# Weight sums and low parts of the first ConvGLU: VectorE subtractions replaced by adding transfers issued by GpSimd

## The chip, the cores and the metric

The kernel runs on one core of one Trainium2 chip. The core has five engines that execute their own instruction lists and wait for each other by semaphores: TensorE (PE in the profile; PEld is its weight load), VectorE (DVE), ScalarE (ACT), GpSimd (POOL) and SyncE (SP), which here only issues transfers. Sixteen DMA engines carry out the transfers. The metric is the device time of one execution in microseconds (us).

## What is computed

The reference is a two-layer model over 512 latent tokens and 256 context tokens of width 1024. Layer 0 mixes tokens by attention, layer 1 by a gated recurrence; each layer ends with a ConvGLU. The change touches the ConvGLU of layer 0, which works on latent and context tokens:

```python
def conv_glu(h, w_up, conv_w, conv_b, w_down):
    gate, val = jnp.split(h @ w_up, 2, axis=-1)
    return (jax.nn.silu(dwconv3(gate, conv_w, conv_b)) * val) @ w_down
```

`w_up` is 1024 x 5632: its first 2816 columns give the gate, the others the value. `dwconv3` is a convolution over three neighbouring tokens. All is float32.

## The kernel before

Every float32 product is made of three products in TensorE's faster float32r format. An operand x is split into a high part, x rounded to float32r, and a low part, x minus the high part; high x high, high x low and low x high are added up in PSUM.

The columns of the ConvGLU are worked through in 22 blocks of 128 (`ft` in `up`, L973). One block needs 128 gate columns and 128 value columns of `w_up`, a pair. With the 1024 rows cut into two halves, the weights of a pair are four blocks: a11 and a12 (gate, first and second half), a21 and a22 (value). The activations are four blocks as well, two halves of the width by two halves of the tokens. The 2 x 2 by 2 x 2 block product is done with seven block products in place of eight, in the manner of Strassen and Winograd: seven sums or differences of weight blocks are multiplied by seven sums or differences of activation blocks (`hs`, prepared once in `combos`, L384), and `gate_pair` (L914) adds the seven results up to the four output blocks. Each block product (`product`, L181) is 12 matmuls of 128 x 128 by 128 x 386.

`load_pair` (L125) prepares the weights of a pair. `load_raw` (L90) issues two transfers on SP's queue, gate and value, into a raw tile `wr` of 128 x 2048. Inside, the nested `total` (L135) makes the four sums s1 to s4 on VectorE, mostly in place in the raw tile, and the nested `parts` (L139) splits each of the seven operands: ScalarE rounds to the high part `wh` (L140), VectorE subtracts to the low part `wl` (L141). Each block is 128 x 512.

Three stocks of tiles set the pace of preparation:

- the raw tiles: two (`wp`, L1306). The weights of the pairs, the weights of the down projection (four transfers a round) and the weights of the conditioning of layer 1 (`wada`, one tile per pair in most pairs, `ada_steps`) take turns in them.
- the operand tiles: six of `wh` and six of `wl` in this stage (four in `ws0`, two in `wsC`), shared by the seven operands of a pair and the operands of the down projection (`load_w`, L99).
- one tile for s1.

The 22 blocks run in six rounds of 3, 4, 4, 4, 3 and 4 (`ROUNDS`). A round first does `up` for its blocks and for the first block of the next round, then the down projection of its blocks: eight output tiles of 128 rows, six matmuls per block and output tile (three products, latent and context tokens apart). After its products, a block is finished on VectorE and ScalarE (convolution, SiLU), with one product with the row factors on GpSimd (L926, `gg` times `R`). The order of the work within each engine is not the program's order: a planner at compile time simulates the program with its own durations and writes a fixed list for every engine, by readiness and priority (`high_priority`, `W_AHEAD`). On the chip each engine executes its list in order.

Of the kernel before, what the change touches and what calls it, by code (L numbers as in the profile page):

```python
# [8 lines left out]
F32 = mybir.dt.float32  # L9
F32R = mybir.dt.float32r  # L10
BF16 = mybir.dt.bfloat16
AF = mybir.ActivationFunctionType
ALU = mybir.AluOpType
# [3 lines left out]
P = 128  # L17
# [51 lines left out]
def f(t):  # L69
    return t.bitcast(F32)  # L70


class Kernel:
# [25 lines left out]
    def load_w(self, parts, cols=False):  # L99
# [23 lines left out]
        return out  # L123

    def load_pair(self, parts, tmp):  # L125


        nc = self.nc
        raw, n = self.load_raw(parts)
        q = n // 4  # L130
        a11, a12, a21, a22 = (raw[:, i * q:(i + 1) * q] for i in range(4))
        s1 = tmp.tile([P, 512], F32, tag="s1", name="s1")[:, 0:q]
        ops = [tuple(t[:, 0:q] for t in self.operand()) for _ in range(7)]

        def total(o, x, y, op):  # L135
            nc.vector.tensor_tensor(o, x, y, op=op)
            return o

        def parts(i, src):  # L139
            nc.scalar.activation(ops[i][0], src, AF.Copy)  # L140
            nc.vector.tensor_tensor(ops[i][1], src, f(ops[i][0]), op=ALU.subtract)  # L141


        with self.tc.high_priority(offset=W_AHEAD):
            parts(0, a11)
            parts(1, a12)
            total(s1, a21, a22, ALU.add)
            s3 = total(a21, a11, a21, ALU.subtract)
            s2 = total(a11, s1, a11, ALU.subtract)
            parts(3, s2)  # L150
            parts(6, s3)
            parts(2, s1)
            parts(5, a22)
            s4 = total(a12, a12, s2, ALU.subtract)
            parts(4, s4)
        return ops

    def wcols(self, w, lo, n):
# [225 lines left out]
    def combos(self, ys, kk, hs, late=False):  # L384

        nc = self.nc
        (b11, b12), (b21, b22) = ys

        def put(i, src):
            nc.scalar.activation(hs[i][:, 0, kk], src, AF.Copy)  # L392
            nc.vector.tensor_tensor(hs[i][:, 1, kk], src, f(hs[i][:, 0, kk]), op=ALU.subtract)

        def diff(o, x, y, eng=nc.vector):
            eng.tensor_tensor(o, x, y, op=ALU.subtract)
            return o

        if late:
            t3 = diff(b22, b22, b12)  # L400
            t4 = diff(b21, b21, b11, nc.gpsimd)
            put(5, diff(b21, t4, t3))
            put(6, t3)
            return
        put(0, b11)
        put(1, b21)
        put(4, b22)
        t1 = diff(b12, b12, b11)
        put(2, t1)
        t2 = diff(b22, b22, t1)  # L410
        put(3, t2)
        yield
        put(5, diff(b21, b21, t2))
        put(6, diff(b11, t2, b11))

    def shifts(self, l, w, hn):
# [497 lines left out]
    def gate_pair(self, ft, ops, hs, G, gg, R, rows, half, tmp, bank):  # L914


        nc = self.nc
        Z, Y, V = (bank(x)[:, 0:half] for x in ("pZ", "pY", "pV"))

        def prod(i, ps, first=False):  # L920
            self.product(ps, ops[i], lambda k: (hs[i][:, 0, k], hs[i][:, 1, k]), 4, first)

        g = (G[:, 1:1 + half], G[:, 1 + half:1 + 2 * half], gg[:, 0:half], gg[:, half:])
        t0, t2 = (tmp.tile([P, half], F32, tag="t", name="t", bufs=2) for _ in range(2))
        add = lambda o, x, y: nc.vector.tensor_tensor(o, x, y, op=ALU.add)  # L925
        times = lambda eng, o, x, y: eng.tensor_tensor(o, x, y, op=ALU.mult)  # L926

        prod(0, Z, True)
        nc.scalar.activation(t0, Z, AF.Copy)
        prod(1, Y, True)  # L930
        add(g[0], t0, Y)
        prod(3, Z)
        nc.scalar.activation(g[2], Z, AF.Copy)
        next(rows, None)
        if ft == 0:
            prod(2, Z)
            nc.scalar.activation(t2, Z, AF.Copy)
            prod(4, Z)
            prod(6, V, True)
            nc.scalar.activation(g[3], V, AF.Copy)  # L940
            prod(5, V)
        else:
            prod(6, V, True)
            nc.scalar.activation(g[3], V, AF.Copy)
            prod(2, Z)
            nc.scalar.activation(t2, Z, AF.Copy)
            prod(5, V)
            prod(4, Z)
        add(g[3], g[3], t2)
        add(g[2], g[2], V)  # L950
        for _ in rows:
            pass

        times(nc.vector, g[0], g[0], R[:, 0:half])
        times(nc.vector, g[1], Z, R[:, half:])
        times(nc.gpsimd, gg, gg, R)
# [496 lines left out]
```

## Time and profile before

| | us |
|---|---|
| median of 3 runs | 1871.61 |
| lowest and highest | 1870.25 and 1875.65 |
| profiled execution | 1872.88 |
| its span, from first to last instruction | 1871.1 |
| first ConvGLU, in the profile | about 446 to 985 |

The page of the profile has six parts: busy time by engine, the span in 40 slices, DMA queues, the chain of work that ended last, the costliest groups of instructions, and DMA issues. The trace behind it answers narrower questions, in the same wording: busy time by windows, groups of instructions in a window, who waited for whom (us in total, times, longest), instructions in order of time. A group's row gives line, engine, operation, output <- inputs, shapes and count, then busy us and mean ns of one, then the engine's idle time before them and what ended it. Busy time of TensorE is modelled, and a few records of matmuls and of other instructions are missing. The slices show where the stages are; the first ConvGLU takes the tenth to the twenty-first.

```profile
PE   6999999998999999999998999999998999999998
...
DVE  5575667466867686766777676777676655455462
ACT  4354555465534252434354333333332443233332
POOL 1233333103201000101013101111110200000000
```

### The profile page before, as it was taken

What the parts mean: (1) busy time and instruction counts of PE and PEld (TensorE: products, weight loads), DVE (VectorE), ACT (ScalarE), POOL (GpSimd) and SP (SyncE); (2) the same over time, 40 slices, a digit from 0 to 9 for tenths busy, and PEclk for the clock granted to TensorE, in tenths of its full rate; (3) what the DMA queues carried; (4) which work ended last, traced back from release to release, by engine and by line L of the source; (5) the groups of instructions that cost most, each with busy time, mean ns of one, the idle gap of its engine ahead of it and who ended that gap; (6) DMA issues with size and microseconds to landing.
All of it is one profiled execution on the core that took longest, in us unless ns stands there. A gap on an engine that the chain in (4) does not pass through costs nothing.

```text
span 1871.1 us, 32302 instructions
## 1 busy us (share of the span) xinstructions
PE 1801.3 (96%) x13326; PEld 1576.9 (84%) x13326; DVE 1214.1 (65%) x2243; ACT 754.7 (40%) x1478; POOL 247.4 (13%) x233
## 2 busy tenths in 40 slices
PE   6999999998999999999998999999998999999998
PEld 4976786787888888989887888988886799899997
DVE  5575667466867686766777676777676655455462
ACT  4354555465534252434354333333332443233332
POOL 1233333103201000101013101111110200000000
PEclk9999999998999999999998999999999999999999
DMA  9204104232333333233313212122220332333321
GB/s 309 66 23 158 47 24 169 68 102 68 124 113 102 113 124 113 91 113 124 113 61 90 58 35 58 35 57 58 57 69 24 90 91 91 90 96 96 92 82 65
DMA packets 204416, 166.44 MB, mean 89 GB/s; under 512 B 5149, under 2 KB 198254, under 8 KB 199150
## 3 DMA queue, kind: packets, MB, share of 16 engines
q1 hardware_dynamic: 196608, 160.47, 27.8%
q10 hardware_dynamic: 7662, 3.92, 0.7%
q8 instruction: 105, 1.72, 0.4%
q14 instruction: 41, 0.34, 0.1%
HBM read 162.27 MB, written 2.10 MB: 88 GB/s over the span
## 4 chain that ended last, share of the span: by engine, by line
PE 87%; DVE 5%; DMA 4%; issue 2%; ACT 1%; POOL 1%; SPq 0%; ACTq 0%; POOLq 0%; DVEq 0%
PE dn L170 15%; PE pd L170 13%; PE pZ L188 8%; PE pf L170 8%; PE pV L188 4%; PE pjq L598 4%; PE pv L170 4%; PE ao L170 4%; PE ho L170 3%; PE pq L170 3%; PE pv L824 2%; PE pt L816 2%; PE ada L309 2%; PE pY L188 2%; PE pgate L170 2%; PE kv L598 2%
## 5 line engine op out<-in xcount | busy, mean ns | idle before, releaser
L117 ACT ACTIVATE wh<-wr 128x512 fp32r<-128x512 f32 (+1 forms) x320 | 193.0, 618 | 452.3 <-DMA wr<-in_ffn_w_up 74.8
L118 DVE TENSOR_TENSOR wl<-wr,wh 128x512 fp32r<-128x512 f32 (+1 forms) x320 | 223.6, 705 | 140.3 <-ACT wh L117 138.3
L170 PE MATMUL dn<-g,wh 128*128 128x512 f32 (+1 forms) x1056 | 263.3, 357 | 2.2 <-ACT g L995 2.2
L170 PE MATMUL pd<-hn,wh 128*128 128x256 f32 (+1 forms) x1408 | 227.3, 284 | 0.9 <-issue 0.9
L170 PEld LDWEIGHTS dn<-g,wh 128*128 128x128 f32 x1056 | 175.4, 189 | 32.7 <-ACT g L995 2.8
L170 PEld LDWEIGHTS pd<-hn,wh 128*128 128x128 f32 x1408 | 194.2, 190 | 2.5 <-issue 2.3
L188 PE MATMUL pZ<-hs,wh 128*128 128x386 f32 x704 | 185.2, 345 | 3.0 <-ACT wh L140 1.5
L170 PE MATMUL dn<-g,wl 128*128 128x512 f32 (+1 forms) x528 | 159.4, 356 | 0.0
L140 ACT ACTIVATE wh<-wr 128x512 fp32r<-128x512 f32 x132 | 81.6, 628 | 167.9 <-DMA wr<-in_ffn_w_up 47.4
L170 PE MATMUL pd<-hn,wl 128*128 128x256 f32 x704 | 141.8, 283 | 0.0
L188 PEld LDWEIGHTS pZ<-hs,wh 128*128 128x128 f32 x704 | 128.0, 190 | 15.7 <-ACT wh L140 4.4
L141 DVE TENSOR_TENSOR wl<-wr,wh 128x512 fp32r<-128x512 f32 x132 | 94.0, 717 | 53.6 <-ACT wh L140 53.5
L170 PE MATMUL pf<-hn,wh 128*128 128x512 f32 (+1 forms) x512 | 119.3, 349 | 9.7 <-DVE xc L1023 8.8
L188 PE MATMUL pZ<-hs,wl 128*128 128x386 f32 x352 | 119.4, 343 | 2.2 <-DVE wl L141 2.2
L926 POOL TENSOR_TENSOR gg<-gg,R 128x772 f32<-128x772 f32 x22 | 53.9, 2449 | 458.3 <-DVE gg L925 446.6
L170 PEld LDWEIGHTS pd<-hn,wl 128*128 128x128 f32 x704 | 109.0, 190 | 0.0
L1023 DVE SCALAR_TENSOR_TENSOR xl<-dn,mod,xl 128x512 f32<-128x512 f32 x72 | 53.9, 748 | 73.7 <-PE dn L170 73.6
L170 PEld LDWEIGHTS dn<-g,wl 128*128 128x128 f32 x528 | 87.4, 188 | 14.8
L170 PEld LDWEIGHTS pf<-hn,wh 128*128 128x128 f32 x512 | 80.9, 192 | 22.5 <-ACT wh L117 9.1
L188 PE MATMUL pV<-hs,wh 128*128 128x386 f32 x352 | 92.2, 341 | 5.0 <-ACT hs L392 5.0
L598 PE MATMUL pjq<-wh,hn 128*128 128x256 f32 x384 | 77.8, 291 | 0.0
L188 PEld LDWEIGHTS pZ<-hs,wl 128*128 128x128 f32 x352 | 66.7, 190 | 6.6 <-DVE gg L925 3.4
(299 smaller groups left out, 3807.1 us busy)
## 6 DMA issues: line engine op xcount, KB each, us to landing
wr<-in_ffn_w_up SPq DMA_DIRECT2D x88, 512.0 KB, 5.1
wada<-in_ada_w SPq DMA_DIRECT2D x40, 1024.0 KB, 4.8
wr<-in_hgrn_w_in SPq DMA_DIRECT2D x40, 512.0 KB, 4.2
ar<-in_ada_w SPq DMA_DIRECT2D x32, 256.0 KB, 7.1
wr<-in_ffn_w_down SPq DMA_DIRECT2D x16, 512.0 KB, 4.1
wr<-in_ffn_w_down SPq DMA_DIRECT2D x8, 896.0 KB, 4.7
wr<-in_attn_w_in SPq DMA_DIRECT2D x6, 1024.0 KB, 8.1
wr<-in_attn_w_out SPq DMA_DIRECT2D x8, 512.0 KB, 4.9
```

The costliest lines, as they stand in the source:

```text
L117: nc.scalar.activation(wh, src, AF.Copy)
L118: nc.vector.tensor_tensor(wl, src, f(wh), op=ALU.subtract)
L140: nc.scalar.activation(ops[i][0], src, AF.Copy)
L141: nc.vector.tensor_tensor(ops[i][1], src, f(ops[i][0]), op=ALU.subtract)
L170: nc.tensor.matmul(o, lhsT=wt, rhs=at[:, t0:t0 + o.shape[1]], start=(first and n == 0 and i == 0), stop=(last and n == len(ks) - 1 and i = ...
L188: self.nc.tensor.matmul(ps, lhsT=wt, rhs=at, start=(first and k == 0 and i == 0), stop=(k == nk - 1 and i == 2), skip_group_check=not first)
L309: nc.tensor.matmul(ps[32 * j:32 * j + 32, 0:512], lhsT=self.cs[:, k, :], rhs=raw[:, j * 512:(j + 1) * 512], start=(k == 0), stop=(k == KT ...
L598: nc.tensor.matmul(out, lhsT=x, rhs=y[:, wk], start=(start and k == 0 and j == 0), stop=(stop and k == KT - 1 and j == 2))
L816: nc.tensor.transpose(pt[:, j * P:(j + 1) * P], pr[j][:, b * P:(b + 1) * P], self.ident)
L824: nc.tensor.matmul(pv[a * HD:(a + 1) * HD, 0:256], lhsT=V[:, tl, g, :], rhs=pT[:, a * 256:(a + 1) * 256], start=(b == 0), stop=(b == len(t ...
L926: times = lambda eng, o, x, y: eng.tensor_tensor(o, x, y, op=ALU.mult)
L1023: nc.vector.scalar_tensor_tensor(x[:, d], o, self.modc(l, v, 5, d), x[:, d], op0=ALU.mult, op1=ALU.add)
```

## The change

`load_pair` no longer uses VectorE. A low part is made in two steps: ScalarE writes the negated high part into `wl` (a Copy with scale -1), and a transfer issued by GpSimd adds the source block to it in place (`dma_start` with `accum_op=ALU.add`). The four sums are adding transfers as well: s3 = a11 + a21 in a tile of its own, which is seeded by a further load of the a11 block from memory on SP's queue; s1 = a21 + a22 in a21; s2 = a11 + s1 in a11; s4 = a12 + s2 in a12. Since a transfer can only add, some of the sums have other signs than before. The signs are made good elsewhere: in `combos` some activation blocks are differences the other way round or are split with a sign of -1 (the low part with `scalar_tensor_tensor` there), and `gate_pair` copies two results with scale -1 and subtracts in place of adding.

```diff
     def load_pair(self, parts, tmp):
...
-        s1 = tmp.tile([P, 512], F32, tag="s1", name="s1")[:, 0:q]
+        s3 = tmp.tile([P, 512], F32, tag="s1", name="s3")[:, 0:q]
         ops = [tuple(t[:, 0:q] for t in self.operand()) for _ in range(7)]
 
-        def total(o, x, y, op):
-            nc.vector.tensor_tensor(o, x, y, op=op)
+        def more(o, x):
+            nc.gpsimd.dma_start(out=o, in_=x, accum_op=ALU.add)
             return o
 
-        def parts(i, src):
+        def parts_(i, src):
             nc.scalar.activation(ops[i][0], src, AF.Copy)
-            nc.vector.tensor_tensor(ops[i][1], src, f(ops[i][0]), op=ALU.subtract)
+            nc.scalar.activation(ops[i][1], f(ops[i][0]), AF.Copy, scale=-1.0)
+            more(ops[i][1], src)
 
         with self.tc.high_priority(offset=W_AHEAD):
-            parts(0, a11)
-            parts(1, a12)
-            total(s1, a21, a22, ALU.add)
-            s3 = total(a21, a11, a21, ALU.subtract)
-            s2 = total(a11, s1, a11, ALU.subtract)
-            parts(3, s2)
-            parts(6, s3)
-            parts(2, s1)
-            parts(5, a22)
-            s4 = total(a12, a12, s2, ALU.subtract)
-            parts(4, s4)
+            nc.sync.dma_start(out=s3.rearrange("p (k m) -> p k m", m=P), in_=parts[0][:, 0:4])
+            parts_(0, a11)
+            parts_(1, a12)
+            more(s3, a21)
+            s1 = more(a21, a22)
+            s2 = more(a11, s1)
+            parts_(3, s2)
+            parts_(6, s3)
+            parts_(2, s1)
+            parts_(5, a22)
+            s4 = more(a12, s2)
+            parts_(4, s4)
         return ops
...
-        def put(i, src):
-            nc.scalar.activation(hs[i][:, 0, kk], src, AF.Copy)
-            nc.vector.tensor_tensor(hs[i][:, 1, kk], src, f(hs[i][:, 0, kk]), op=ALU.subtract)
+        def put(i, src, sign=1.0):
+            nc.scalar.activation(hs[i][:, 0, kk], src, AF.Copy, scale=sign)
+            if sign > 0:
+                nc.vector.tensor_tensor(hs[i][:, 1, kk], src, f(hs[i][:, 0, kk]), op=ALU.subtract)
+            else:
+                nc.vector.scalar_tensor_tensor(hs[i][:, 1, kk], src, sign, f(hs[i][:, 0, kk]), op0=ALU.mult, op1=ALU.subtract)
...
-        put(2, t1)
+        put(2, t1, -1.0)
...
-        put(3, t2)
+        put(3, t2, -1.0)
...
-        nc.scalar.activation(g[2], Z, AF.Copy)
+        nc.scalar.activation(g[2], Z, AF.Copy, scale=-1.0)
...
-        add(g[3], g[3], t2)
-        add(g[2], g[2], V)
+        less(g[3], t2)
+        less(g[2], V)
```

More of the change, by code (lines that the diff above doesn't have):

```diff
@@ L401, in combos @@
             t4 = diff(b21, b21, b11, nc.gpsimd)
-            put(5, diff(b21, t4, t3))
+            put(5, diff(b21, t3, t4))
             put(6, t3)
@@ L408, in combos @@
         t1 = diff(b12, b12, b11)
-        put(2, t1)
+        put(2, t1, -1.0)
         t2 = diff(b22, b22, t1)
-        put(3, t2)
+        put(3, t2, -1.0)
         yield
-        put(5, diff(b21, b21, t2))
+        put(5, diff(b21, t2, b21))
         put(6, diff(b11, t2, b11))
@@ L925, in gate_pair @@
         add = lambda o, x, y: nc.vector.tensor_tensor(o, x, y, op=ALU.add)
+        less = lambda o, x: nc.vector.tensor_tensor(o, o, x, op=ALU.subtract)
         times = lambda eng, o, x, y: eng.tensor_tensor(o, x, y, op=ALU.mult)
@@ L939, in gate_pair @@
             prod(6, V, True)
-            nc.scalar.activation(g[3], V, AF.Copy)
+            nc.scalar.activation(g[3], V, AF.Copy, scale=-1.0)
             prod(5, V)
@@ L943, in gate_pair @@
             prod(6, V, True)
-            nc.scalar.activation(g[3], V, AF.Copy)
+            nc.scalar.activation(g[3], V, AF.Copy, scale=-1.0)
             prod(2, Z)
```

## The prediction

> **What bounds the kernel now.** The first view is the page's head and its table of engines.
>
> ```profile
> span 1871.1 us, 32302 instructions
> PE 1801.3 (96%) x13326; PEld 1576.9 (84%) x13326; DVE 1214.1 (65%) x2243; ACT 754.7 (40%) x1478; POOL 247.4 (13%) x233
> ```
>
> TensorE is busy for 96% of the span. The average says little about one stage, so the second view is the table of windows, for the first ConvGLU (the only stage the change touches) and for the 26 us before it, in which its first weights come in.
>
> ```profile
> core 0: us, PE busy (x) PEld busy (x) DVE busy (x) ACT busy (x) POOL busy (x), PEclk, DMA share, GB/s
> 420.00:446.00 26.00, 18.43 (x98) 14.59 (x96) 17.95 (x29) 15.07 (x37) 12.36 (x17) 0.86 0.27 82
> 446.00:985.00 539.00, 531.77 (x3010) 478.95 (x3009) 388.51 (x653) 222.54 (x394) 61.38 (x29) 1.00 0.34 106
> ```
>
> In these 539 us TensorE is idle for 539 - 531.77 = 7.2 us, at full clock, and VectorE is busy for 72%. The third view is what TensorE waited for there, in us in total, times, longest.
>
> ```profile
> PE pZ L188 <- DVE wl L141: 2.2, 3, 1.6
> ...
> PE pZ L188 <- ACT wh L140: 1.5, 4, 0.4
> PE pY L188 <- ACT wh L140: 0.6, 1, 0.6
> ```
>
> All that operands cost TensorE is 4.3 us. So the most that a faster preparation can bring is 7.2 us (0.4%) in this stage, however many VectorE instructions go. The question is whether the new path can still keep TensorE fed.
>
> **What goes and what comes.** The groups of instructions of the stage give the old path's durations.
>
> ```profile
> L141 DVE TENSOR_TENSOR wl<-wr,wh 128x512 fp32r<-128x512 f32 x124 | 88.1, 716 | 49.4 <-ACT wh L140 49.3
> ...
> L140 ACT ACTIVATE wh<-wr 128x512 fp32r<-128x512 f32 x124 | 76.6, 628 | 158.6 <-DMA wr<-in_ffn_w_up 42.9 <-PE dn L170 38.2 <-DVE wr L136 33.8
> ...
> L926 POOL TENSOR_TENSOR gg<-gg,R 128x772 f32<-128x772 f32 x22 | 53.9, 2449 | 458.3 <-DVE gg L925 446.6 <-DVE hn L423 11.7
> ...
> L136 DVE TENSOR_TENSOR s<-wr 128x512 f32<-128x512 f32 x20 | 13.8, 689 | 2.4 <-DMA wr<-in_ffn_w_up 2.3
> ```
>
> There are 22 pairs. VectorE loses 7 subtractions and 4 sums a pair: 22 x (7 x 0.716 + 4 x 0.689) = 171 us, down to 40% of the stage. TensorE hid nearly all of it, so I credit nothing. ScalarE gains 7 copies a pair, 22 x 7 x 0.628 = 97 us: 222.5 becomes 319, 59% of 539, and TensorE hides it too; without that cover it would be 4.4 us a pair. GpSimd gains 11 adding transfers a pair beside its one 2.4 us product, and SP one 256 KB load (the seed of s3). The sign changes in combos and gate_pair keep the number of instructions; two of seven low parts change their form, which I cost at nothing (the stage's other work hides it).
>
> What matters is the **chain of one pair**. Before, the four sums and the last split are six short steps. Now the transfer s3 += a21 must land before a21 is overwritten by a21 += a22; that must land before a11 += s1, that before a12 += s2, then ScalarE makes high part and seed, and the fifth transfer adds the low part of operand 4. With L for issue to landing of one adding transfer of 256 KB, from landing of the weights to release of the raw tile: 5 L + 2 x 0.628 = 5 L + 1.3 us. How long is L? This trace shows no transfer from GpSimd and none that adds. The nearest rows are the page's queue and issues of 256 KB, and SP's issue times and landings of the stage's weights:
>
> ```profile
> q1 hardware_dynamic: 196608, 160.47, 27.8%
> ...
> ar<-in_ada_w SPq DMA_DIRECT2D x32, 256.0 KB, 7.1
> ...
> xs<-in_x ACTq DMA_DIRECT2D x8, 256.0 KB, 2.7
> ```
>
> ```profile
> L95 SPq DMA_DIRECT2D wr<-in_ffn_w_up x40: 367/472/1403, 456.8 to 928.0; - x40
> ...
> DMA to landing us min/median/max: 2.9/4.2/5.3
> ```
>
> A plain load of 256 KB lands in 2.7 us when the queue is quiet and in 7.1 us in a burst. From the queue's row, 160.47 MB in 27.8% of 1871.1 us, the 16 engines move 308 GB/s, or 0.85 us for 0.262 MB. An adding transfer must also read its destination: one more pass, 2.7 + 0.85 + 0.47 (issue) = 4.0 us as the quiet end; the busy end is 7.1 + 0.47 = 7.6 us. I take the middle, L = 6 us, because eleven such transfers a pair make the queue far busier than the 0.34 share of before, and keep 2.7 and 7.6 for the range (and below 2.7 no reason shows a gain, since TensorE is already full).
>
> The Trainium skill, "DMA: Bandwidth & Descriptors", section "Anatomy of one DMA — SWDGE (gpsimd) path", gives a transfer issued by GpSimd about 2.0 us plus its bytes at 436 GB/s. By that rule L would be an estimated 2.6 us; the sum by it would come out as that of the first rival below, and no row here shows such a transfer.
>
> How long may a pair take? The SP queue's order in time shows the cycle of the two raw tiles, which the stage's weights share with the ada weights:
>
> ```profile
> 634.86 0.99 SPq L95 DMA_DIRECT2D wr<-in_ffn_w_up  x2
> 641.83 0.34 SPq L307 DMA_DIRECT2D wada<-in_ada_w  x1
> 651.89 0.99 SPq L95 DMA_DIRECT2D wr<-in_ffn_w_up  x2
> 660.91 0.34 SPq L307 DMA_DIRECT2D wada<-in_ada_w  x1
> 667.57 0.99 SPq L95 DMA_DIRECT2D wr<-in_ffn_w_up  x2
> ```
>
> Weights that enter one tile at 634.86 leave it at 660.91 to ada weights, which stay to 667.57, 6.7 us. The tile turns in 32.7 us, two pairs, 16.35 us each, and that is TensorE's own pace: seven products of 2.13 us and the ada rows.
>
> ```profile
> 451.40 2.13 PE pZ L188 x12
> ...
> 605.70 28.10 PE dn L170 x160
> ```
>
> The new minimum of a turn is 4.2 (landing) + 5 L + 1.3 + 6.7, for two pairs half of it each: **6.1 + 2.5 L a pair**. TensorE is kept fed up to L = (16.35 - 6.1) / 2.5 = 4.1 us. At L = 6 a pair takes 21.1 us, 4.75 us more. About one pair a round is prepared under the down products (28 us and more in one piece, second row), so six of 22 stay covered: 16 x 4.75 = 76 us. The six operand tiles are not the limit: 6 x 16.35 / 7 = 14.0 us each, while high part, seed, transfer and product need 1.3 + 6 + 2.1 = 9.4. The single s3 buffer is not either: load, add, ScalarE and add take 2.7 + 6 + 1.3 + 6 = 16.0 us, just under the pair's 21.1.
>
> GpSimd executes in order, and its product waits long:
>
> ```profile
> 651.57 2.27 POOL L926 TENSOR_TENSOR gg<-gg,R 128x772 f32<-128x772 f32 x1 [47.99 <-DVE gg L925]
> 668.35 2.23 POOL L926 TENSOR_TENSOR gg<-gg,R 128x772 f32<-128x772 f32 x1 [14.51 <-DVE gg L925]
> ```
>
> Today nothing stands behind it. Now the next pair's transfers do, and ScalarE's copies wait for those, then TensorE. I count half its mean duration, 1.2 us, in the 16 uncovered pairs: 20 us. The waiting itself (14.5 us before the second row) is the price if the order is bad; it is kept for the second rival.
>
> The first pair has no cover:
>
> ```profile
> 433.66 0.63 ACT L140 ACTIVATE wh<-wr 128x512 fp32r<-128x512 f32 x1 [2.08 <-DMA wr<-in_ffn_w_up]
> ```
>
> ```profile
> L141 DVE TENSOR_TENSOR wl<-wr,wh x124: 674/689/1577, 452.7 to 948.3; 128x512 fp32r<-128x512 f32 x124
> ```
>
> From its weights' landing at 433.66 to the end of the low part that starts at 452.7 it takes 19.7 us; the new chain takes 5 x 6 + 1.3 = 31.3, so 12 us more.
>
> **Sum**: 76 + 20 + 12 = 108 us. The profiled execution took 1872.9 us (its span 1871.1), 1.3 us above the median 1871.6: 1872.9 + 108 = **1981 us**, 5.8% slower.
>
> **Rivals.** (1) Not slower: the transfers hide. If L stays below 4.1 us, the two raw tiles still turn faster than TensorE: at L = 2.7 a pair needs 6.1 + 6.75 = 12.9 us against 16.35, and the first pair 14.8 against 19.7. Then the time stays at 1873 us, or at best loses the 7.2 idle us: 1866. For it: the 2.7 us row, and VectorE's relief. Against: that row neither reads its destination nor shares the queue with ten more.
>
> (2) GpSimd's in-order queue lets only one pair run at a time: its list waits inside a pair for each landing and then for the product. A pair then takes 5 x 6 + 1.3 + 2.4 = 33.7 us, 17.4 more; 16 x 17.4 + 12 = 290 us, 2163 us. For it: the long waits before the product. Against: other transfers of the same and of the next pair could be placed in the gaps.
>
> (3) The 16 DMA engines become the bound. 22 x 11 x 0.262 = 63.4 MB at 308 GB/s are 206 us in one pass, the seeds 19 us, and the present share 0.34 x 539 = 183 us. With two passes per add: 412 + 19 + 183 = 614 us, 75 more than 539, which the forecast holds already; with three: 820 us, 281 more, 2154 us. For it: reading two and writing one. Against: none of the rows shows an add.
> The Trainium skill, "DMA: Bandwidth & Descriptors", section "Issuing engines are not separate DMA queues", says that transfers issued by SP, ScalarE and GpSimd run on the same 16 engines; the trace of before, with no transfer from GpSimd, can't show it.
>
> (4) The change doesn't do what it says: the sums stay on VectorE. Nothing in the diff supports that; 1873 us.
>
> **Numbers.** Forecast (1900 to 2070) 0.42; rival 1 0.17; rival 2 0.25; rival 3 0.14; rival 4 0.02. Of rival 1 some 0.05 end faster by over 0.3% (5.6 us, about what a measurement of this kernel can tell from no change), 0.05 within it, and 0.07 a little slower, between L = 4.1 and 4.6; with rival 4, same is 0.07. Slower: 0.88. The range runs from 1880 to 2200: it holds the forecast with both ends of L (at 7.6 the sum is 16 x 8.75 + 20 + 20 = 180, 2053 us) and rivals 2 and 3 at their prices, and leaves out about 0.12 below and 0.08 above. The forecast's own range is 1900 to 2070.
>
> **What would show it.** Right: TensorE's waits in the stage lead to operands (wl behind a DMA, wh behind a DMA on a raw tile); the adding transfers land in 4 to 7.6 us; the SP rows of the up weights stand 20 us or more apart; VectorE's share falls to about 40%, ScalarE's rises to about 59%; the stages after 985 us are the same, shifted. Wrong: landings under 4 us with TensorE full (rival 1); GpSimd idle before its product while the next pair's transfers stand behind it (rival 2); a DMA share near 1 (rival 3). Should the compiler's order of the work change much, the working by raw tiles fails whatever L is.

## The result, and the profile after

The kernel after takes 2060.3 us (median of 4 runs, 2057.7 to 2061.6) against 1871.4 us: ratio 1.1003, 95% interval 1.0983 to 1.1023, 189 us slower. The forecast was 1981 us, with a range of 1880 to 2200.

First the page of the profile after: head, engines, the queue of the adding transfers, and four kinds of issues with their median from issue to landing.

```profile
span 2058.3 us, 32875 instructions
...
PE 1864.0 (91%) x13326; PEld 1617.5 (79%) x13326; DVE 1069.6 (52%) x2001; ACT 838.8 (41%) x1632; POOL 443.4 (22%) x475
...
q0 software_dynamic: 34848, 63.45, 18.3%
...
wl<-wr POOLq DMA_DIRECT2D x132, 256.0 KB, 5.1
wr<-wr POOLq DMA_DIRECT2D x66, 256.0 KB, 4.3
...
s<-in_ffn_w_up SPq DMA_DIRECT2D x22, 256.0 KB, 5.1
...
s<-wr POOLq DMA_DIRECT2D x22, 256.0 KB, 4.1
wl<-s POOLq DMA_DIRECT2D x22, 256.0 KB, 6.1
```

There are 132 + 66 + 22 + 22 = 242 adding transfers, eleven for each of 22 pairs. They land after 4 to 6 us by these medians. Now the table of windows for the stage, which lasts from 446 to about 1172 us instead of 985:

```profile
446.00:1172.00 726.00, 590.49 (x2991) 515.43 (x2990) 251.74 (x426) 300.33 (x536) 246.81 (x257) 0.90 0.78 170
```

The stage grew by 726 - 539 = 187 us, which is the whole loss. By this view it has two parts. TensorE is idle for 726 - 590.5 = 135.5 us, where it was 7.2 (+128). And the same products take 590.5 us where they took 531.8 (+59), since the granted clock fell from 1.00 to 0.90. VectorE did lose its work: 251.7 us instead of 388.5. Its relief buys nothing.

The third view, what TensorE waited for in the stage (us in total, times, longest):

```profile
PE ada L312 <- DMA wada<-in_ada_w: 41.0, 12, 8.9
PE pZ L191 <- DMA wl<-wr: 24.8, 14, 5.2
PE pZ L191 <- ACT wh L141: 17.8, 6, 5.9
PE pZ L191 <- ACT t L936: 12.3, 4, 3.6
...
```

Where 4.3 us were lost on operands, TensorE now waits for adding transfers on low parts, for high parts whose source is late, and most of all for the `wada` weights. These last come in a raw tile that a pair has to leave first, so they may be a symptom; an experiment below asks.

What SP's queue waited for shows how the tiles come free. Before, L307 issued the `wada` loads and L95 the weights, and VectorE's subtractions released the raw tiles:

```profile
SPq L307 <- DVE wl L141: 93.5, 12, 14.9
...
SPq L95 <- DVE wl L141: 46.8, 6, 12.6
```

After, L310 issues the `wada` loads, L95 the weights, L147 the seed load of s3:

```profile
SPq L310 <- DMA wl<-wr: 205.2, 24, 18.9
SPq L147 <- DMA wl<-s: 138.6, 18, 12.9
SPq L95 <- DMA wl<-wr: 75.4, 14, 15.0
...
```

Now a raw tile is released by the landing of an adding transfer, and SP waits 205 + 75 = 281 us for such releases, where it waited 94 + 47 = 140 us for VectorE. The new seed load makes SP wait another 139 us, because the only s3 tile is still in use, and the next loads stand behind it in the same queue.

Last, GpSimd's list in order of time, for two pairs in the middle of the stage (start, duration, instruction, and in brackets the idle time before it and what ended that):

```profile
700.54 1.22 POOL L137 DMA_DIRECT2D s<-wr  x1
...
705.58 0.87 POOL L137 DMA_DIRECT2D wr<-wr  x1 [2.93 <-PE pZ L191]
...
716.01 0.87 POOL L137 DMA_DIRECT2D wr<-wr  x1 [7.81 <-DMA wl<-wr]
716.58 2.18 POOL L933 TENSOR_TENSOR gg<-gg,R 128x772 f32<-128x772 f32 x1
718.39 1.22 POOL L137 DMA_DIRECT2D wl<-s  x1
723.79 0.87 POOL L137 DMA_DIRECT2D wr<-wr  x1 [4.18 <-DMA wr<-wr]
...
729.60 1.56 POOL L137 DMA_DIRECT2D s<-wr  x1
...
735.40 0.87 POOL L137 DMA_DIRECT2D wr<-wr  x1 [1.73 <-DMA s<-wr]
738.69 0.87 POOL L137 DMA_DIRECT2D wl<-s  x1 [2.42 <-issue]
739.25 1.21 POOL L137 DMA_DIRECT2D wr<-wr  x1
...
749.75 0.87 POOL L137 DMA_DIRECT2D wr<-wr  x1 [1.26 <-DMA wl<-wr]
754.14 0.86 POOL L137 DMA_DIRECT2D s<-wr  x1 [3.52 <-DMA wr<-in_ffn_w_up]
```

`s<-wr` is s3, the first sum of a pair; the three `wr<-wr` are s1, s2 and s4. Over the 22 pairs, s3 of the next pair is issued after s4 of this one in 19 of 21 successions, and just ahead of it in the other two. So the chains of two pairs stand one behind the other in the list, 29.1 and 24.5 us apart here, where TensorE needs a pair every 16.35 us. Inside a pair the list stops for landings: 7.81 us before s2, because a low part's transfer must have read a11 before s2 may overwrite it, and 4.18 us before s4. Over the stage it waits longest for ScalarE's seeds of the low parts, and in six cases s3 had to wait for the weights of its pair:

```profile
POOL wl L137 <- ACT wl L142: 126.5, 73, 14.9
...
POOL s L137 <- DMA wr<-in_ffn_w_up: 45.1, 6, 14.7
```

So the list waits by turns for ScalarE, for landings and for weights.

The DMA engines' share of 0.78 is a mean as well. Two stretches in which pairs are prepared, and between them one of down products:

```profile
560.00:620.00 60.00, 43.10 (x198) 38.31 (x199) 15.65 (x31) 28.92 (x53) 26.64 (x29) 0.82 1.00 208
640.00:680.00 40.00, 40.00 (x228) 36.34 (x227) 23.77 (x40) 17.33 (x29) 8.28 (x8) 1.00 0.55 135
720.00:780.00 60.00, 44.67 (x201) 38.73 (x204) 18.67 (x30) 30.44 (x55) 26.42 (x28) 0.83 0.98 206
```

TensorE idles where the share is 1.00 and 0.98, and not where it is 0.55. This alone does not tell whether the engines are what is late, as the pairs are prepared in the same stretches.

### The profile page after: what moved, and what is told of

Same layout as the page of the kernel before. It is cut to its first block, busy times and chain, and to the rows that moved or that the text cites. A ratio compares the mean times of both kernels' runs of the same rounds, so it can differ in the third digit from the quotient of the medians.

```text
span 2058.3 us, 32875 instructions
## 1 busy us (share of the span) xinstructions
PE 1864.0 (91%) x13326; PEld 1617.5 (79%) x13326; DVE 1069.6 (52%) x2001; ACT 838.8 (41%) x1632; POOL 443.4 (22%) x475
## 3 DMA queue, kind: packets, MB, share of 16 engines
q0 software_dynamic: 34848, 63.45, 18.3%
## 4 chain that ended last, share of the span: by engine, by line
PE 44%; DMA 9%; issue 3%; DVE 2%; ACT 2%; POOL 1%; POOLq 0%; SPq 0%; DVEq 0%; ACTq 0%
PE pd L173 12%; PE dn L173 8%; PE pf L173 7%; PE pv L173 3%; DMA wr<-wr 2%; PE pq L173 2%; DMA wl<-wr 2%; PE ho L173 2%; PE pgate L173 2%; PE pZ L191 1%; DMA wr<-in_ffn_w_up 1%; PE lv L1139 1%; PE U L1204 1%; DMA s<-wr 1%; DMA wada<-in_ada_w 1%
## 5 line engine op out<-in xcount | busy, mean ns | idle before, releaser
L173 PE MATMUL dn<-g,wh 128*128 128x512 f32 (+1 forms) x1056 | 268.3, 362 | 12.8 <-ACT wh L117 9.5
L191 PE MATMUL pZ<-hs,wh 128*128 128x386 f32 x704 | 204.9, 376 | 33.9 <-ACT wh L141 17.8
L191 PEld LDWEIGHTS pZ<-hs,wh 128*128 128x128 f32 x704 | 142.3, 213 | 53.0 <-ACT wh L141 24.6
L141 ACT ACTIVATE wh<-wr 128x512 fp32r<-128x512 f32 x132 | 80.4, 624 | 207.1 <-DMA wr<-wr 132.9
L137 POOL DMA_DIRECT2D wl<-wr x132 | 125.7, 1013 | 156.8 <-ACT wl L142 137.5
L191 PE MATMUL pZ<-hs,wl 128*128 128x386 f32 x352 | 131.5, 377 | 27.8 <-DMA wl<-wr 27.8
L191 PEld LDWEIGHTS pZ<-hs,wl 128*128 128x128 f32 x352 | 74.3, 211 | 37.8 <-DMA wl<-wr 34.2
L191 PE MATMUL pV<-hs,wh 128*128 128x386 f32 x352 | 99.4, 366 | 3.2 <-ACT hs L395 1.3
L137 POOL DMA_DIRECT2D wr<-wr x66 | 59.1, 895 | 184.6 <-DMA wr<-wr 49.5
L142 ACT ACTIVATE wl<-wh 128x512 fp32r<-128x512 f32 x154 | 94.4, 624 | 2.0
```

What stands on the lines that cost most here:

```text
L137: nc.gpsimd.dma_start(out=o, in_=x, accum_op=ALU.add)
L142: nc.scalar.activation(ops[i][1], f(ops[i][0]), AF.Copy, scale=-1.0)
L173: nc.tensor.matmul(o, lhsT=wt, rhs=at[:, t0:t0 + o.shape[1]], start=(first and n == 0 and i == 0), stop=(last and n == len(ks) - 1 and i = ...
L191: self.nc.tensor.matmul(ps, lhsT=wt, rhs=at, start=(first and k == 0 and i == 0), stop=(k == nk - 1 and i == 2), skip_group_check=not first)
```

## The experiments

Three theories stood at the start. **Chain**: the adding transfers depend on each other and on landings; what costs is the number of landings in line. **Load**: what costs is the amount of transfers on the DMA engines. **List**: the fixed lists of GpSimd and ScalarE hold ready work behind work that waits. A fourth came up, **tile**: the operand tiles or the raw tiles run out. All runs, each against the kernel before on the same chip:

| kernel | us | ratio, interval |
|---|---|---|
| after | 2060.3 | 1.1003 (1.0983 to 1.1023) |
| low parts alone by transfers | 1946.4 | 1.0384 (1.0303 to 1.0466) |
| sums alone by transfers | 1930.4 | 1.0299 (1.0263 to 1.0335) |
| ScalarE's copies, no transfers | 1884.4 | 1.0049 (1.0024 to 1.0074) |
| after, plain copies for the additions | 1962.7 | 1.0471 (1.0441 to 1.0501) |
| after, s2 and s4 on VectorE | 2017.4 | 1.0756 (1.0736 to 1.0775) |
| after, gg x R on VectorE | 2053.3 | 1.0945 (1.0886 to 1.1003) |
| after, `wada` work ahead of the stage | 2105.3 | 1.1222 (1.1155 to 1.1290) |
| after, operand tiles two to one | 2090.8 | 1.1144 (1.1084 to 1.1205) |
| low parts alone, operand tiles two to one | 1909.0 | 1.0178 (1.0159 to 1.0196) |
| before, operand tiles two to one | 1862.7 | 0.9920 (0.9892 to 0.9948) |
| the same again, 5 runs | 1863.8 | 0.9934 (0.9920 to 0.9947) |
| before, with needless transfers | 1995.2 | 1.0637 (1.0618 to 1.0656) |

The kernels before beside them took 1874 to 1876 us. Differences below are against those. Where a run is compared with after itself, the kernels before beside the two lie up to 4.5 us apart, so such a difference is good to some 5 us.

### The parts of the change one by one

Low parts alone: the four sums go back to VectorE and the seed load is left away.

```diff
+        def total(o, x, y):
+            nc.vector.tensor_tensor(o, x, y, op=ALU.add)
+            return o
...
-            nc.sync.dma_start(out=s3.rearrange("p (k m) -> p k m", m=P), in_=parts[0][:, 0:4])
...
-            more(s3, a21)
-            s1 = more(a21, a22)
-            s2 = more(a11, s1)
+            total(s3, a11, a21)
+            s1 = total(a21, a21, a22)
+            s2 = total(a11, a11, s1)
...
-            s4 = more(a12, s2)
+            s4 = total(a12, a12, s2)
```

> The seven low parts stay adding transfers seeded by ScalarE; the four sums go back to VectorE, without the extra load for s3. Chain theory (a raw tile is held while four dependent adds and a last one land, two raw tiles turn in that time): what is left of the chain is 5.2 landing + 4 x 0.7 + 1.3 + one add 5.1 = 14.4 us, less than the 25 us that a raw tile is held before, so TensorE sets the pace again: 1870 to 1890 us. Load theory (the 16 DMA engines, busy for 0.78 of the stage, make every landing late): 7 of 11 adds remain, so 7/11 of the 189 us: about 1990 us. List theory (GpSimd's and ScalarE's fixed lists wait behind each other): 7 of 11 issues and all copies remain, 1950 to 1990 us.

Sums alone: the low parts go back to VectorE.

```diff
-            nc.scalar.activation(ops[i][1], f(ops[i][0]), AF.Copy, scale=-1.0)
-            more(ops[i][1], src)
+            nc.vector.tensor_tensor(ops[i][1], src, f(ops[i][0]), op=ALU.subtract)
```

> The four sums stay adding transfers with the load that seeds s3; the seven low parts go back to VectorE. Chain theory: the chain loses only its last add, 5.2 + 4.1 + 3 x 4.3 + 1.3 = 23.5 us at least against 28.6, so at least half of the loss stays: 1965 to 2040 us. Load theory: 4 of 11 adds, 1940 us. List theory: 4 of 11 issues and no extra copies, 1900 to 1940 us.

ScalarE's copies alone: the sums on VectorE as in the first edit, and the low part is added there too.

```diff
-            more(ops[i][1], src)
+            nc.vector.tensor_tensor(ops[i][1], f(ops[i][1]), src, op=ALU.add)
```

> No transfer from GpSimd: ScalarE still writes the negated high parts, VectorE adds the source to them in place and makes the four sums. It takes the 97 us of ScalarE's extra copies by themselves. Chain and load theory: hidden, 1868 to 1885 us. List theory as far as it blames ScalarE's 14 copies a pair: 1900 us or more.

Measured: 1946, 1930 and 1884 us, that is +72, +56 and +10. Low parts by transfers cost, although they make no chain of sums; the chain theory's 1870 to 1890 for them is wrong, and so is its 1965 to 2040 for the sums. The low parts come nearest to the lower end of the list theory, 1950; the sums lie in its range and 10 us under the 1940 of the load theory. Spread evenly, the four chained sums with their seed load cost 14 us each, the seven low parts (72 - 10) / 7 = 9. The two together, 128, are less than the 189 of the whole change: 61 us come only when both are there. The 10 us belong to ScalarE's 154 further copies, which the prediction had hidden, together with the other signs and the other order of the sums, which that kernel has as well.

### The adding against the transferring

The same lists on every engine, with plain copies where after adds:

```diff
-            nc.gpsimd.dma_start(out=o, in_=x, accum_op=ALU.add)
+            nc.gpsimd.dma_start(out=o, in_=x)
```

> As the changed kernel, but the eleven transfers a pair copy and do not add (the additions are left out); every engine's list is the same. Chain theory: each landing loses the pass that reads the destination, about 0.7 us; five of them are 3.5 us of a turn, 1.8 us a pair, 22 pairs: 2020 us. Load theory: the engine time of the transfers, 377 us, halves, and the share of the stage falls from 0.78 to about 0.55: most of the loss goes, 1900 to 1960 us. List theory: no change, 2050 to 2060 us.

Measured: 1962.7 us, 98 less than after. That is the load theory's number (1900 to 1960) but for 3 us; the chain theory's 2020 and the list theory's 2050 to 2060 are wrong. The row of the line that issues them, first in after, then with copies:

```profile
L137 POOL DMA_DIRECT2D wl<-wr x132: 860/872/1571, 397.6 to 1137.0; - x132
...
DMA to landing us min/median/max: 3.3/4.7/9.4
```

```profile
L137 POOL DMA_DIRECT2D wl<-wr x132: 537/540/771, 397.2 to 1038.6; - x132
...
DMA to landing us min/median/max: 2.2/2.9/8.1
```

An adding transfer lands 1.8 us later than a copy of the same 256 KB and holds GpSimd for 0.87 us in place of 0.54 (the middle of the three numbers, in ns). So half of the loss goes with the adding. Spread over the 16 pairs that the prediction left uncovered, 98 us are 6.1 us a pair, or 3.4 times 1.8, as if each of those pairs paid for three to four landings in line. That lies between the 2.5 of the forecast (two pairs side by side) and the 5 of a strictly serial chain. It is an upper figure, as the issue time and the clock are in the 98 us too, and so is the time of the DMA engines, whose share of the stage falls from 0.78 to 0.63. The run shows what the adding costs, not by which of these ways. The other half stays even with copies.

The Trainium skill, "DMA: Bandwidth & Descriptors", section "Anatomy of one DMA — SWDGE (gpsimd) path", gives 2.0 us plus bytes at 436 GB/s, for 256 KB an estimated 2.6 us. The copies agree with it (2.2 at the least, 2.9 in the middle), the adding transfers don't (3.3 and 4.7).

### Two links of the chain on VectorE

```diff
+        def total(o, x, y):
+            nc.vector.tensor_tensor(o, x, y, op=ALU.add)
+            return o
...
-            s2 = more(a11, s1)
+            s2 = total(a11, a11, s1)
...
-            s4 = more(a12, s2)
+            s4 = total(a12, a12, s2)
```

> The kernel after with s2 and s4 made by VectorE again (one addition each); s3, s1 and the seven low parts stay adding transfers (nine of the eleven). Chain theory (the pairs' chains of dependent transfers run one after another in GpSimd's list; period of a pair about 5 landings + 3.7 us): the chain loses two landings of about 4.5 us and gains two additions of 0.7 us, so a pair takes some 7.6 us less in 16 pairs: 1940 to 1970 us. Load theory (what counts is the number of adding transfers on GpSimd and on the DMA engines): nine elevenths of 189 us stay, about 155: 2015 to 2035 us.

Measured: 2017.4 us, 43 less than after. That is the load theory's number (2015 to 2035), not the chain's (1940 to 1970). But what VectorE waited for in the stage shows that the chain did not get two landings shorter:

```profile
DVE wr L141 <- DMA wl<-wr: 107.8, 17, 15.7
```

L141 is the new addition. In 17 cases it stood for 6.3 us in the mean, up to 15.7, until a low part's transfer had read the block that the sum overwrites. The low parts' landings are links of the chain as well, and VectorE is now held up by them. So the run does not decide between the theories: the chain as it was written down left out these links.

### Transfers that nobody waits for

The kernel before, with 13 transfers a pair from a finished gate tile to memory:

```diff
-        times(nc.gpsimd, gg, gg, R)
+        times(nc.vector, gg, gg, R)
...
+            if not lat_only:
+                for _ in range(13):
+                    nc.gpsimd.dma_start(out=self.dr.tile([P, n], F32, tag="dr", name="dr"), in_=f(g2[:, 0]))
```

> The kernel before with 13 transfers a pair that nobody needs, issued by GpSimd from a finished gate tile to memory (128 x 770 float32, 394 KB each; about as much time of the DMA engines per pair as the eleven adding transfers take); the product gg x R goes to VectorE so that nothing else stands in GpSimd's list behind them. Load theory (the traffic on the DMA engines and in on-chip memory by itself slows weights, engines or TensorE's clock): 1930 to 1990 us or more, with lower clock and longer landings. Chain theory (traffic is hidden, dependence is what costs): 1865 to 1885 us.

Measured: 1995.2 us, +120, with the product gg x R on VectorE as a second change. Traffic that nobody waits for can cost about as much as that; the DMA engines' share of the stage is 0.77, as in after. But by which way? The landings of the weights issued at L95 in the stage, here:

```profile
L95 SPq DMA_DIRECT2D wr<-in_ffn_w_up x40: 367/472/5380, 455.1 to 1038.5; - x40
...
DMA to landing us min/median/max: 3.8/10.8/30.8
```

and in after, up to 1000 us:

```profile
DMA to landing us min/median/max: 3.2/4.4/7.9
```

Before they were 2.9/4.2/5.3. The needless transfers come 13 in a row, and a weight load that meets such a row lands after up to 30.8 us. In after the weights land practically as before. So this way of losing time exists, and the weights of after do not show it; the run refutes the claim that traffic is always hidden, and does not show that traffic is the cause in after. The Trainium skill, "DMA: Bandwidth & Descriptors", section "Issuing engines are not separate DMA queues", says that transfers of SP and GpSimd share the same 16 engines; the 30.8 us agree.

### The list's other work, and the raw tiles

The product gg x R on VectorE:

```diff
-        times(nc.gpsimd, gg, gg, R)
+        times(nc.vector, gg, gg, R)
```

> The changed kernel, with the product of gate and value results with the row factors on VectorE in place of GpSimd, so that GpSimd's list holds adding transfers alone in the stage. List theory: the 68 us in which GpSimd stands before this product, with the next pair's transfers behind it, go, and half or more of them reach the end: 1990 to 2025 us. Chain, tile and load theory: GpSimd's list is not what is late: 2040 to 2065 us.

Measured: 2053.3 us, 7 less than after, or 12 if each is set against its own kernel before; the intervals of the two ratios overlap, so this is not told from nothing. The list theory's 1990 to 2025 is wrong. GpSimd's waits before that product, 68.4 us in 13 cases, are hardly paid for:

```profile
POOL gg L933 <- DVE gg L932: 68.4, 13, 16.8
```

This is after's row of GpSimd's waits in the stage.

The `wada` loads and products of three rounds, in front of the stage instead of within it:

```diff
-        self.ap_, self.ap_tag = Rp, "acc"
-        self.ffn(0, hs, R, rows, False, tmp, acp, bk, gp, done0, (x for r in (0, 1, 2) for x in self.ada_steps(1, r, bk, "ps", 512)))
+        self.ap_, self.ap_tag = tmp, "nt"
+        for r in (0, 1, 2):
+            for _ in self.ada_steps(1, r, bk, "ps", 512):
+                pass
+        self.ffn(0, hs, R, rows, False, tmp, acp, bk, gp, done0)
```

> The changed kernel, with the 24 loads and products for the conditioning of layer 1 ahead of the stage, so that the raw tiles serve the ConvGLU's weights alone there. The stage's own length is to be read, since the loads cost time of their own ahead of it. Chain and tile theory: a pair's turn loses the 9 us that ada weights hold a raw tile, 4.5 us a pair: the stage is 726 - 22 x 4.5 - 24 (the products) = about 600 us. Load theory: the 25 MB of these loads are 82 us of the engines' 566: stage about 640 us. List theory: the stage loses only the products and TensorE's wait for these loads, 24 + 41: about 660 us.

Measured: 2105.3 us, 45 more. What counts here is the stage itself, from its first product to the point 886 us ahead of the end of the span, first in after, then here:

```profile
427.80:1172.00 744.20, 604.25 (x3056) 527.38 (x3053) 262.79 (x441) 314.83 (x572) 260.97 (x279) 0.90 0.77 169
```

```profile
511.30:1214.00 702.70, 571.40 (x2857) 518.68 (x2856) 241.62 (x411) 305.04 (x549) 254.93 (x267) 0.90 0.74 148
```

The first product comes 83.5 us later, since the loads and their products now stand ahead of it. Of the 41.5 us that the stage is shorter, 33 are products that left, and TensorE's idle time is 131 us instead of 140. That makes 684 us of the 726, more than the 600, 640 or 660 that the theories expected. So the largest row of TensorE's waits, 41 us for `wada`, was for the most part a symptom: without these loads in the raw tiles the pairs are late all the same.

### The operand tiles

`operand` (L84) takes tiles in turn from the pools in its list, `ws0` with four and `wsC` with two. So the two tiles of `wsC` get every second operand. With the list `ws0`, `wsC`, `ws0` the share follows the sizes:

```diff
+        keep = self.wsp
+        self.wsp = [self.ws0, next(p for p in keep if p is not self.ws0), self.ws0]
         self.ffn(0, hs, R, rows, False, tmp, acp, bk, gp, done0, (x for r in (0, 1, 2) for x in self.ada_steps(1, r, bk, "ps", 512)))
+        self.wsp = keep
```

This edit was put into after, into before, and into the kernel with low parts alone.

> The changed kernel, with the operands of the first ConvGLU shared out two to one over the stocks of four and two operand tiles, where it was one to one. Tile theory (new: one to one, each of the two tiles must turn in two times 2 operands, 9.3 us at TensorE's pace, and an operand now needs 1.3 + 4.7 + 2.1 plus its waits; this adds the 12 us that a raw tile is held beyond its chain of transfers): all six tiles share, 14 us each, the raw tiles are held 5 to 10 us less, 2.5 to 5 us a pair: 1950 to 2010 us. Load theory: the same bytes at the same pace, 2040 to 2060 us. List theory of GpSimd: 2040 to 2060 us.

> The kernel before with the same two to one share of the operand tiles: the control. TensorE is idle for only 7 us in the stage, so all theories say 1866 to 1876 us.

> The kernel with low parts alone by adding transfers (sums on VectorE), its operand tiles taken two to one from the pools of four and of two tiles, in place of one to one. Tile theory (the +72 us of that kernel come from operands that hold their tiles longer, and the pool of two is the first to run out): 1885 to 1915 us. Order theory (they come from the late transfers themselves, behind others in GpSimd's list or slow to land): 1935 to 1960 us.

Measured: 2090.8 us in after (30 more), 1862.7 in before (13 less than beside it), 1909.0 with low parts alone (37 less). In that last kernel the waits of the products for low parts shrink. First the row with equal shares, then with two to one:

```profile
PE pZ L194 <- DMA wl<-wr: 20.4, 13, 3.8
```

```profile
PE pZ L194 <- DMA wl<-wr: 8.8, 8, 2.4
```

So there the tiles are about half of the +72, as the tile theory had it (1885 to 1915). With one-to-one shares a tile of `wsC` has 2 x 16.35 / 3.5 = 9.3 us for an operand, and the prediction's own need was 9.4 us. In after the same edit makes it worse: ScalarE's waits for the in-place sums (`wr<-wr`: s1, s2 and s4) up to 1160 us, first in after, then with the edit,

```profile
ACT wh L141 <- DMA wr<-wr: 127.9, 35, 10.9
```

```profile
ACT wh L141 <- DMA wr<-wr: 204.0, 44, 15.3
```

grow by 76 us. Why the other shares make the sums later was not found; no theory had a loss there (the highest bound was 2060), nor a gain in before (1866 to 1876).

The edit in before is the one version that beats both kernels, so it was run again:

> The kernel before with its operand tiles taken two to one from the pools of four and two in the first ConvGLU, timed again. If its gain of 0.8% is real: 1860 to 1866 us, ratio 0.990 to 0.995. If it was chance: 1869 to 1874 us, ratio 0.998 to 1.001.

Measured: 1863.8 us, ratio 0.9934 (0.9920 to 0.9947): the gain is real, about 0.7%.

## Why the prediction was right in kind and short in size

**The bound.** Right for this change. TensorE was full, and VectorE's 137 us less in the stage gained nothing. But 7.2 us was not the most that any change could bring: the two-to-one tiles gain 12 to 13 us. In the profile of the first such run layer 1's products `pf` start at 994.6 us, in before at 1003.8, so the 7.2 us of the window up to 985 do not hold all the idle time around the stage.

**L, the landing.** Mis-sized, on the high side: 6 us assumed, 4.7 measured. The quiet end, put together from a plain load, one more pass and the issue, was 4.0, and the point up to which TensorE would be fed 4.1. The engine time of a transfer came out right: 18.3% of 2058.3 us over 242 transfers is 1.56 us, against two passes of 0.85, 1.70.

**The turn of the raw tile, 6.1 + 2.5 L.** This step failed. With the measured L it gives 17.9 us a pair, 1.5 more than 16.35, or 24 us in 16 pairs, where the step had 76. The stage lost 187. The "2.5" halves a chain of five landings because two raw tiles would hold two pairs that proceed side by side. GpSimd's list hardly lets them: s3 of the next pair stands behind s4 of this one in 19 of 21 cases, with the low parts and `gg` between, and the pairs shown above are 29.1 and 24.5 us apart. That is the order that rival 2 described, at a smaller L; no run changed the list's order alone, so what it costs is argued and not shown. Its own formula gives 5 x 4.7 + 1.3 + 2.4 = 27.2 us and (27.2 - 16.35) x 16 + 12 = 186 us, near the measured 189. But this agreement proves little: the same formula with the copies' 2.9 us gives 18.2 us and 42 us, where 88 were measured, and with s2 and s4 on VectorE it was to give 90 to 120 us less than after, where 43 were measured.

**The sum.** With the measured L it would have been 24 + 20 + 12 = 56 us, or 1929 us. That 2060 lies within 1880 to 2200, and even within the forecast's own 1900 to 2070, is luck as far as the forecast's working goes: the range was wide enough for another mechanism.

**The single s3 tile is not the limit, 16.0 us.** Failed. The sum left out what stands in GpSimd's list between the add into s3 and the transfer that frees it: 718.39 - 700.54 = 17.9 us in one pair above and 738.69 - 729.60 = 9.1 in the other. With 5.1 us for the load ahead of it and 6.1 for the last landing that makes 20 to 29 us, more than TensorE's 16.35 us a pair and about the 24 to 29 us that a pair takes there. SP's 138.6 us of waiting at L147 show that the tile comes free late. A second s3 tile was not tried.

**The six operand tiles are not the limit, 14.0 against 9.4 us.** Failed where low parts alone are made by transfers (37 us there): the share of the pool of two is 9.3 us, not 14.0. In after itself the other shares cost 30 us more, and why stays open.

**GpSimd's product, 20 us.** Mis-sized: 7 to 12 us, within the noise. **ScalarE's copies, nothing.** Mis-sized: at most 10 us. **The first pair, 12 us.** Misread and not seen. The split at 433.66 us follows weights issued at 428.80, those of the second pair; the first pair's were issued at 391.74 us, and it was prepared under the last products of the attention (`ao`). TensorE's first products of the stage start no later. The two rows are those of before and of after.

```profile
428.68 0.62 PE L188 MATMUL pZ<-hs,wh 128*128 128x386 f32 x2
```

```profile
427.79 0.62 PE L191 MATMUL pZ<-hs,wh 128*128 128x386 f32 x2
```

**Not in the sum at all: the clock.** 59 of the 187 us are products that take longer at a granted clock of 0.90. The row of the stage with sums alone, and then with low parts alone:

```profile
446.00:1044.10 598.10, 546.05 (x2994) 485.89 (x2993) 347.55 (x569) 218.45 (x390) 123.43 (x111) 0.97 0.55 140
```

```profile
446.00:1052.30 606.30, 551.34 (x2998) 489.20 (x2997) 298.10 (x507) 300.07 (x536) 175.72 (x173) 0.97 0.68 159
```

The clock is 0.97 where TensorE idles for 598.1 - 546.1 = 52 and 606.3 - 551.3 = 55 us, and 0.90 at 135. The Trainium skill, "TensorE: Matmul & The Clock Gate", section "What's actually happening", says that the clock falls to half after an idle window of about 3.4 us; waits of up to 8.9 us in after and a clock below 1 agree with that, though no run here separates the idle time from other causes.

**Rival 3, the DMA engines as the bound.** Not settled. For it: its sign, a share near 1, does show in the stretches that lose time (1.00 and 0.98 above), and the load theory came within 3 us for the copies and held for s2 and s4 on VectorE. Against it: the load theory missed the low parts alone by 44 us, the weights land after 4.4 us in the middle, 4.2 before, and with copies 88 us are lost at a share of 0.63. No run took time from the DMA engines without shortening the landings too. **Rival 1 and rival 4** are out by the result.

What stays open is how the loss divides. Shown: about half of it (98 us) goes with the adding; some 10 us at most each with `gg` and with ScalarE's copies; little with the `wada` loads. Shown for low parts alone: half of +72 by the operand tiles. The rest lies between the landings that release raw tiles, the s3 tile, the order of GpSimd's list and the time of the DMA engines, and no run changed one of these by itself.

## What to carry to other kernels

A vector instruction that is replaced by a transfer turns 0.7 us into a landing of 4.7, and each landing is also a release: ask of every tile that the transfer reads or writes who waits to reuse it, and of every instruction queued behind it. Two buffers overlap two chains only as far as the issuing engine's list interleaves them, which is argued here and not shown by a run; read the list's order before halving a latency. A share of 0.78 over a stage can be 1.00 in the stretches that matter; read it there. And where tiles are taken in turn from two pools, the smaller pool can be the limit, not the sum of the tiles.

## What was not expected of the hardware

- An adding transfer of 256 KB within on-chip memory takes 1.56 us of the 16 engines' time against 0.82 for a copy (10.1% of 1958.9 us over 242), 4.7 us to land against 2.9, and 0.87 us of GpSimd to issue against 0.54.
- Behind thirteen transfers of 385 KB in a row a weight load of SP's queue landed after as much as 30.8 us.
- With TensorE idle for a fifth of a stage its granted clock there was a tenth lower: 7.2 idle of 539 us at 1.00, 135.5 of 726 at 0.90.
